# Two buffers for the key tiles of the first attention part, and norm row factors by way of DRAM

## The chip, the cores and the metric

The kernel runs on one core of one Trainium2 chip. The core has five engines that run side by side and are held together by semaphores: TensorE (PE in the profile, its weight loads PEld), VectorE (DVE), ScalarE (ACT), GpSimd (POOL) and SyncE (SP). Here every DMA is issued from SP's queue, in the order in which the program stands there. The metric is the device time of one execution in microseconds (us), as the median of several runs.

## The reference

One layer of a streaming encoder, in float32, for 2048 prompt tokens and 32 sample tokens of width 1024:

```
z  = rmsnorm(x, g_attn) @ w_in            # 3072 columns: q, k, v of two head groups
oa = differential attention, 4 heads:     # softmax(q1 k1) - lam * softmax(q2 k2), chunk-causal, T5 bias
ob = band attention, 8 heads of 64:       # each 64-frame chunk sees itself and the 8 chunks before
h  = x + concat(rmsnorm(oa) * c, rmsnorm(ob)) @ w_out
h  = h + square(relu(rmsnorm(h) @ w_up)) @ w_down
h  = h + sigmoid(h @ w_ple_gate) * (p @ w_ple_proj)
y  = rmsnorm(h)                           # also returned: the new keys and values of both groups
```

The first norm is `x * rsqrt(mean(x*x) + eps) * g`. The factor `rsqrt(...)` is one number for each token, the row factor of this text.

## The kernel before

The tokens are worked on in four blocks of 512 (the last has the 32 sample tokens as well, 544). Activations stand transposed, features on partitions and tokens along the free axis. Each float32 product is made of three fp32r matmuls, from a high and a low part of both operands (`mm3`, lines 215 to 217); ACT makes the high part (line 180) and POOL or DVE the low one (lines 165, 175, 186).

`prep` (line 358) takes a block in tiles of 128 tokens. For each it loads x, squares it on ACT with a running sum, transposes it on TensorE into PSUM tiles `xp` (line 377), takes the high and low parts with the gain `g_attn` (lines 382, 383), copies the plain transposed x away (line 386) and stores it. The norm's factor is not multiplied into the activations. It is worked out in `rsqrt` (lines 219 to 231) into a column of `rcol`, one token on each partition, and used after the projections: the value tiles have tokens on partitions and take `rcol` as the scale of their ACT copy (line 421), while the query and key tiles have tokens along the free axis and need the factors as a row that is the same on all partitions. This is the tile `rb[b]` (`rbt` in the profile, three buffers), read in lines 475 and 480. It is made by a TensorE transpose of the column broadcast to 128 columns (`rp`, line 391), in the PSUM ring that `prep` is given, and an ACT copy into `rb[b]` (line 392), once for each token tile, 17 times in all.

`attn_a` (line 571) is the differential attention. It runs twice: once over queries 0 to 1023 (`JA0`, with `self.small` set, pool `a0`), once over the rest and the sample (`JA1`, pool `a1`). For each of 4 heads it loads a bias tile `ba` (one buffer; a POOL memset follows its load, line 329), the head's keys `kt` (tag `ka`, in two DMAs) and then, for each 256 queries, q tiles, the scores `s` (line 632), the near block's bias and maximum (line 641) or the far block's maximum (line 638), the exponentials (line 646), the weighted difference (lines 668, 669), the transposes `tpp` (line 704), the copies `pH` and `pL` (711, 712), the product with v (`o`, lines 718 to 720) and a norm by column sums (`ss`, lines 729, 730). In the first run `ka` has one buffer of 1024 keys, in the second two of 2048. `attn_b` is the band attention, also in two runs (scores `sb` line 802, transposes `tpb` line 817, product `ob` line 842).

`run` writes this down as: `prep` of blocks 0 and 1 with the first value tiles; the first group's projection for them; `attn_a` over `JA0`; the second group's projection for block 0; `prep(2)` woven into the projection of block 1; the first run of `attn_b`; `prep(3)` woven into the projection of block 2; and so on to the second `attn_b`, the first group's projection of blocks 2 and 3, `attn_a` over `JA1`, the output projection, the MLP and the gate. The order on each engine is not the written one: a scheduler with a timing model of its own takes the instructions by priority and by readiness of their data and buffers, and so mixes the attention with the projections. A change of a buffer count or of a producer can change that order far behind its place. On each engine and on SP's queue the order is fixed once the program is built.

Of the kernel before, what the change touches and what calls it, by code (L numbers as in the profile page):

```python
# [12 lines left out]
F32 = mybir.dt.float32  # L13
F32R = mybir.dt.float32r
AF = mybir.ActivationFunctionType
# [4 lines left out]
P = 128  # L20
D = 1024
SP = 2048
SS = 32
T = SP + SS
# [16 lines left out]
BN = {0: 512, 1: 512, 2: 512, 3: 544}  # L41
# [3 lines left out]
def toks(b):  # L45
    out = []
    for i in range(4):
        out.append((i * P, P))
    if b == 3:
        out.append((512, SS))  # L50
    return out
# [91 lines left out]
class Kern:  # L143
# [197 lines left out]
    def scratch(self):  # L341
        self.xT = self.dram([P, 8, T], F32, "xT")
        self.qS = self.dram([8, 2, 64, 9, 2, 256], F32, "qS")
        self.kS = self.dram([8, 2, P, KC], F32, "kS")
        self.vS = [self.dram([KC, D], F32, "vSa"), self.dram([KC, D], F32, "vSb")]
        self.oT = self.dram([P, 8, T], F32, "oT")
        self.hS = self.dram([P, 8, T], F32, "hS")
        self.rS = self.dram([P, T], F32, "rS")
        self.rB = self.dram([P, T], F32, "rB")
        self.pS = self.dram([P, 2, 2, T], F32, "pS")  # L350

# [6 lines left out]
    def prep(self, b, acts, pp, mm, tag, first=None):  # L358
        nc = self.nc
        aH, aL = acts[b]  # L360
        for i, (c0, n) in enumerate(toks(b)):
            t0 = 512 * b + c0
            x = pp.tile([P, D], F32, tag="x", name="x")
            self.dma(x[:n], self.xsrc(t0, n))
            if first is not None:
                first()
                first = None
            xt = pp.tile([P, 8, P], F32, tag="xt", name="xt")
            st = pp.tile([P, 1], F32, tag="st", name="st")
            nc.scalar.activation(  # L370
                xt[:n].rearrange("p a b -> p (a b)"), x[:n], AF.Square, accum_out=st[:n]
            )
            for h in range(2):
                xp = mm.tile([P, 4, P], F32, tag=tag, name="xp")
                for k in range(4):
                    kk = 4 * h + k
                    nc.tensor.transpose(xp[:, k, :n], x[:n, kk * P : kk * P + P], self.ident[:n, :n])
                for k in range(4):
                    kk = 4 * h + k
                    g = self.g_attn[:, kk : kk + 1]  # L380
                    hi, lo = aH[:, kk, c0 : c0 + n], aL[:, kk, c0 : c0 + n]
                    nc.scalar.activation(hi, xp[:, k, :n], AF.Copy, scale=g)
                    nc.vector.scalar_tensor_tensor(
                        lo, xp[:, k, :n], g, hi.bitcast(F32), op0=ALU.mult, op1=ALU.subtract
                    )
                nc.vector.tensor_copy(xt[:, 4 * h : 4 * h + 4, :n], xp[:, :, :n])
            self.dma(self.xT[:, :, t0 : t0 + n], xt[:, :, :n])
            r = self.rcol[:n, 4 * b + i : 4 * b + i + 1]
            self.rsqrt(pp, st[:n], 1, 1.0 / D, EPS, nc.vector, "r1", n, out=r)
            rp = mm.tile([P, 512], F32, tag=tag, name="rp")  # L390
            nc.tensor.transpose(rp[:, :n], r.broadcast_to([n, P]), self.ident[:n, :n])
            nc.scalar.activation(self.rb[b][:, c0 : c0 + n], rp[:, :n], AF.Copy)
            yield

    def ktok(self, b):
# [175 lines left out]
    def attn_a(self, js, pool, ps_s, ps_t, ps_o):  # L571
        nc = self.nc
        last = 8 in js
        nk = SP if last else 256 * (js[-1] + 1)
        for g in range(4):
            ba = self.bias_a(pool, g)
            kt = pool.tile([P, 2, 1024 if self.small else SP], F32R, tag="ka", bufs=1 if self.small else 2, name="ka")
            if last:
                ks = pool.tile([P, 2, PAST + SS], F32R, tag="ks", bufs=1, name="ks")
            for hl in range(2):  # L580
                src = self.kS[g, hl].rearrange("(m r) c -> r m c", m=2)
                for c0 in range(0, nk, 1024):
                    c1 = min(c0 + 1024, nk)
                    self.dma(kt[64 * hl : 64 * hl + 64, :, c0:c1], src[:, :, c0:c1])
                if last:
                    self.dma(ks[64 * hl : 64 * hl + 64], src[:, :, SP:KC])
            for j in js:
                self.attn_a_pair(g, j if j < 8 else None, kt if j < 8 else ks, ba, pool, ps_s, ps_t, ps_o)
# [981 lines left out]
```

## Time and profile before

| | |
|---|---|
| median of 3 runs | 3191.57 us (3189.75 to 3192.46) |
| profiled execution | 3197.78 us, span 3196.0 us |
| granted TensorE clock, mean | 0.977 |
| TensorE / weight loads busy | 3037.6 us (95%) / 2694.5 us (84%) |
| DVE / ACT / POOL busy | 1851.6 / 1885.5 / 1887.4 us (58%, 59%, 59%) |
| DMA | 521.61 MB, mean 163 GB/s |

A group's row has line, engine, operation, tile written and tiles read, form and count, then busy time with the mean of one in ns, then the engine's idle time just before and what ended it. A row of a wait has who waited for whom, the total in us, how often, and the longest. A row of a tile has the shortest, median and longest duration in ns, and the start of the first and the last. A row of DMA issues has the number, the size of one and the median time from issue to landing. A row of a stretch has its two ends, its length, then each engine's busy time with its instructions, the granted clock, the DMA engines' busy share and GB/s.

### The profile page before, as it was taken

How to read it: one execution, taken by the hardware profiler on the slowest of the kernel's cores; microseconds unless marked ns; L12 is line 12 of the kernel's file. 1: busy time of each engine (PE TensorE's matmuls, PEld its weight loads, DVE VectorE, ACT ScalarE, POOL GpSimd, SP SyncE). 2: the span in 40 equal slices, each digit the busy share in tenths (PEclk: the TensorE clock that was granted, in tenths of full speed). 3: DMA queues.
4: the chain of work that ended last, by engine and by line, in shares of the span. 5: the costliest groups of instructions: out<-in, count | busy, mean ns of one | idle time of the engine just before them, and what ended most of it. 6: DMA issues, size and time to landing. Idle time of an engine off the chain costs nothing.

```text
span 3196.0 us, 53414 instructions
## 1 busy us (share of the span) xinstructions
PE 3037.6 (95%) x18265; PEld 2694.5 (84%) x18265; DVE 1851.6 (58%) x4448; ACT 1885.5 (59%) x4166; POOL 1887.4 (59%) x2572
## 2 busy tenths in 40 slices
PE   8998989999999998999999999998999999899998
PEld 7787877899987787877788888877888888899998
DVE  5157774544454554666765666435577665776663
ACT  5256775766665764676665666554555555554445
POOL 4466546333335544565554555677787778867674
PEclk9998999999999999999999999999999999999999
DMA  8787767977688745555554534446524334233331
GB/s 267 237 242 224 208 191 237 251 227 206 199 244 227 209 130 134 149 165 138 170 158 139 148 111 119 126 147 216 182 86 147 106 99 127 93 100 108 92 114 55
DMA packets 512505, 521.61 MB, mean 163 GB/s; under 512 B 37949, under 2 KB 393601, under 8 KB 512233
## 3 DMA queue, kind: packets, MB, share of 16 engines
q1 hardware_dynamic: 512232, 518.19, 55.2%
q8 instruction: 145, 2.38, 0.3%
q14 instruction: 128, 1.04, 0.1%
HBM read 412.08 MB, written 109.95 MB: 163 GB/s over the span
## 4 chain that ended last, share of the span: by engine, by line
PE 68%; DMA 12%; DVE 10%; ACT 4%; issue 3%; POOL 2%; SPq 1%; DVEq 0%; ACTq 0%; POOLq 0%
PE dps L215 6%; PE dps L216 6%; PE dps L217 6%; PE ups L215 6%; PE ups L216 6%; PE ups L217 6%; PE s L632 3%; PE qps L215 3%; PE qps L216 3%; PE qps L217 3%; DMA oraw<-oT 2%; PE ob L842 2%; PE tpb L817 1%; PE tpp L704 1%; DMA wr<-w_up 1%
## 5 line engine op out<-in xcount | busy, mean ns | idle before, releaser
L175 POOL TENSOR_TENSOR wl<-wr,wh 128x256 fp32r<-128x256 f32 x648 | 474.5, 764 | 333.6 <-ACT wh L180 328.0
L180 ACT ACTIVATE piece<-wr 128x512 fp32r<-128x512 f32 x412 | 252.9, 626 | 289.0 <-PE ups L216 144.0
L175 POOL TENSOR_TENSOR piece<-wr,piece 128x256 fp32r<-128x256 f32 x416 | 336.4, 834 | 103.2 <-ACT piece L180 87.8
L180 ACT ACTIVATE wh<-wr 128x1024 fp32r<-128x1024 f32 x228 | 240.8, 1057 | 198.5 <-PE qps L216 51.7
L165 POOL TENSOR_TENSOR wl<-wr,wh 128x256 fp32r<-128x256 f32 x264 | 197.9, 781 | 185.8 <-ACT wh L180 180.4
L215 PE MATMUL ups<-cs,piece 128*128 128x256 f32 (+1 forms) x896 | 257.3, 288 | 7.8 <-ACT piece L180 6.1
L217 PE MATMUL ups<-cs,piece 128*128 128x256 f32 (+1 forms) x896 | 257.4, 287 | 5.6 <-POOL piece L175 5.6
L216 PE MATMUL ups<-cs,piece 128*128 128x256 f32 (+1 forms) x896 | 256.6, 286 | 0.5 <-DVE cs L186 0.5
L216 PE MATMUL dps<-ul,piece 128*128 128x272 f32 (+1 forms) x768 | 247.7, 324 | 1.3 <-DVE ul L186 1.3
L217 PE MATMUL dps<-uh,piece 128*128 128x272 f32 (+1 forms) x768 | 247.5, 324 | 1.2 <-POOL piece L165 1.2
L215 PE MATMUL dps<-uh,piece 128*128 128x272 f32 (+1 forms) x768 | 246.2, 324 | 1.0 <-DVE h L1124 0.8
L165 POOL TENSOR_TENSOR piece<-wr,piece 128x256 fp32r<-128x256 f32 x280 | 223.5, 829 | 25.1 <-ACT piece L180 24.3
L1124 DVE TENSOR_TENSOR h<-h,dps 128x272 f32<-128x272 f32 (+1 forms) x384 | 190.8, 515 | 81.5 <-PE dps L217 80.5
L215 PE MATMUL qps<-aH,wh 128*128 128x512 f32 (+1 forms) x640 | 230.8, 361 | 5.8 <-DVE ql L475 4.3
L215 PE MATMUL dps<-uh,wh 128*128 128x512 f32 x512 | 209.5, 409 | 20.8 <-ACT wh L180 7.2
L216 PE MATMUL qps<-aL,wh 128*128 128x512 f32 (+1 forms) x640 | 229.2, 358 | 0.0
L217 PE MATMUL qps<-aH,wl 128*128 128x512 f32 (+1 forms) x640 | 228.4, 357 | 0.0
L1083 DVE TENSOR_TENSOR h<-h,dps 128x512 f32<-128x512 f32 x256 | 174.2, 682 | 82.3 <-PE dps L217 77.6
L632 PE MATMUL s<-ka,q 128*128 128x512 f32 (+3 forms) x768 | 188.6, 349 | 19.4 <-DMA ka<-kS 10.0
L215 PE MATMUL ups<-cH,wh 128*128 128x512 f32 x512 | 202.7, 396 | 0.5 <-DVE h L1083 0.4
L216 PE MATMUL dps<-ul,wh 128*128 128x512 f32 x512 | 202.1, 395 | 0.0
L217 PE MATMUL dps<-uh,wl 128*128 128x512 f32 x512 | 202.1, 395 | 0.0
(298 smaller groups left out, 9764.7 us busy)
## 6 DMA issues: line engine op xcount, KB each, us to landing
wr<-w_up SPq DMA_DIRECT2D x128, 512.0 KB, 4.1
wr<-w_down SPq DMA_DIRECT2D x128, 512.0 KB, 3.7
wr<-w_in SPq DMA_DIRECT2D x74, 512.0 KB, 4.6
q<-qS SPq DMA_DIRECT2D x128, 256.0 KB, 5.2
v<-vSa SPq DMA_DIRECT2D x64, 512.0 KB, 3.9
ka<-kS SPq DMA_DIRECT2D x32, 512.0 KB, 7.8
wr<-w_out SPq DMA_DIRECT2D x32, 512.0 KB, 5.0
wr<-w_ple_gate SPq DMA_DIRECT2D x32, 512.0 KB, 4.1
```

The costliest lines, as they stand in the source:

```text
L165: nc.gpsimd.tensor_tensor(out[:, sl], a[:, sl], b[:, sl], op=op)
L175: nc.gpsimd.tensor_tensor(out[:, sl], a[:, sl], b[:, sl], op=op)
L180: nc.scalar.activation(hi, raw, AF.Copy)
L215: nc.tensor.matmul(ps, lh, rh, start=start and i == 0, stop=False)
L216: nc.tensor.matmul(ps, lh, rl, start=False, stop=False)
L217: nc.tensor.matmul(ps, ll, rh, start=False, stop=stop and i == n - 1)
L632: nc.tensor.matmul(s, q[:, m, hl, P * qi : P * qi + nr], kt[:, m, k0 - kb : k0 - kb + n], start=hl == 0, stop=hl == 1)
L704: nc.tensor.transpose(tp[:kn, x, :nr], w[:nr, P * i : P * i + kn], self.ident[:nr, :nr])
L817: nc.tensor.transpose(tp[:kn, x, :nr], e[:, P * (x0 + x) : P * (x0 + x) + kn], self.ident[:nr, :nr])
L842: nc.tensor.matmul(o[:, qa:qb], vt, pt[:kn, i - kfirst, qa:qb], start=x == 0 and y == 0, stop=x == len(order) - 1 and y == 1,)
L1083: nc.vector.tensor_tensor(hv, hv, ps, op=ALU.add)
L1124: nc.vector.tensor_tensor(hv, hv, ps, op=ALU.add)
```

## The change

Two edits. The key tile of the first `attn_a` run gets two buffers, as the second run has. And the rows `rb[b]` are no longer made by transposes: when a block's last token tile is done, the block's columns of `rcol` are written to a DRAM vector `rR` (one token after the other, so in pieces of 4 bytes), and one DMA reads 512 (or 544) factors of it back, repeated on all 128 partitions. The lines behind the first added line move by one, those behind the second edit by eight.

```diff
@@ scratch
+        self.rR = self.dram([T], F32, "rR")
@@ prep
             self.rsqrt(pp, st[:n], 1, 1.0 / D, EPS, nc.vector, "r1", n, out=r)
-            rp = mm.tile([P, 512], F32, tag=tag, name="rp")
-            nc.tensor.transpose(rp[:, :n], r.broadcast_to([n, P]), self.ident[:n, :n])
-            nc.scalar.activation(self.rb[b][:, c0 : c0 + n], rp[:, :n], AF.Copy)
+            if i == len(toks(b)) - 1:
+                self.dma(
+                    self.rR[512 * b : 512 * b + 512].rearrange("(i p) -> p i", p=P), self.rcol[:, 4 * b : 4 * b + 4]
+                )
+                if b == 3:
+                    self.dma(self.rR[SP:T].rearrange("(i p) -> p i", p=SS), self.rcol[:SS, 16:17])
+                self.dma(
+                    self.rb[b][:, : BN[b]],
+                    self.rR[512 * b : 512 * b + BN[b]].unsqueeze(0).broadcast_to([P, BN[b]]),
+                )
             yield
@@ attn_a
-            kt = pool.tile([P, 2, 1024 if self.small else SP], F32R, tag="ka", bufs=1 if self.small else 2, name="ka")
+            kt = pool.tile([P, 2, 1024 if self.small else SP], F32R, tag="ka", bufs=2, name="ka")
```

## The prediction

> **What bounds the kernel now.** I read the page first, then busy time by stretch, then TensorE's waits, then the rows that the change touches.
>
> ```profile
> span 3196.0 us, 53414 instructions
> PE 3037.6 (95%) x18265; PEld 2694.5 (84%) x18265; DVE 1851.6 (58%) x4448; ACT 1885.5 (59%) x4166; POOL 1887.4 (59%) x2572
> PEclk9998999999999999999999999999999999999999
> PE 68%; DMA 12%; DVE 10%; ACT 4%; issue 3%; POOL 2%; SPq 1%; DVEq 0%; ACTq 0%; POOLq 0%
> ```
>
> TensorE is busy for 95% of the span and holds 68% of the chain that ended last. So what counts is (a) TensorE work removed, (b) TensorE's idle time, (c) stretches with a lowered clock. Busy time by stretch (TensorE, weight loads, DVE, ACT, POOL, then granted clock, DMA share, GB/s):
>
> ```profile
> 0.00:180.00 180.00, 160.99 (x912) 135.83 (x913) 60.95 (x169) 71.57 (x181) 73.31 (x110) 0.98 0.78 249
> 180.00:530.00 350.00, 311.92 (x1848) 276.46 (x1848) 231.62 (x732) 237.21 (x683) 216.55 (x313) 0.92 0.74 213
> 530.00:1000.00 470.00, 449.69 (x3154) 416.86 (x3153) 231.40 (x832) 311.59 (x662) 193.26 (x306) 0.99 0.81 232
> 1000.00:2010.00 1010.00, 970.69 (x4991) 818.75 (x4992) 604.67 (x1467) 648.52 (x1464) 539.83 (x765) 0.98 0.53 149
> 2010.00:3196.00 1186.00, 1144.30 (x7365) 1046.59 (x7364) 723.00 (x1250) 616.65 (x1179) 864.40 (x1080) 0.98 0.39 120
> ```
>
> The weakest stretch is 180 to 530 us: the first differential attention part, the second group's projection and the preparation of token blocks 2 and 3 run into each other there. TensorE is idle for 38.1 of 350 us at a clock of 0.92. Both edits work in this stretch or before it.
>
> **The change part by part.** TensorE's waits that the edits touch, or that stand beside them, are these, of the whole run:
>
> ```profile
> PE s L632 <- DMA ka<-kS: 10.0, 4, 3.8
> PE ob L842 <- ACT pHb L826: 7.2, 7, 2.3
> PE rp L391 <- DVE xt L386: 7.1, 6, 2.1
> PE tpp L704 <- DVE e L669: 4.3, 5, 1.4
> PE ss L729 <- DVE sh L182: 3.5, 4, 1.8
> PE ss L729 <- DVE rz L657: 2.3, 1, 2.3
> PE rp L391 <- DVE rcol L230: 2.0, 3, 1.1
> ```
>
> *Row factors, what goes.* 17 transposes on TensorE and 17 copies on ACT:
>
> ```profile
> L391 PE MATMUL rp<-ident,rcol x17: 237/323/477, 10.7 to 526.1; 128*128 128x128 f32 x16, 32*128 32x32 f32 x1
> L392 ACT ACTIVATE rbt<-rp x17: 188/277/313, 11.9 to 526.4; 128x128 f32<-128x128 f32 x16, 128x32 f32<-128x32 f32 x1
> ```
>
> 17 at a median of 0.323 is 5.5 us of TensorE, all of it on the bounding engine: **-5.6** (their exact sum is 5.6). The copies are 17 x 0.277 = 4.7 us on an ACT that is busy 59%: I give them nothing.
>
> Before these transposes TensorE idles 7.1 + 2.0 = 9.1 us. The 2.0 us wait for the factor itself goes. The 7.1 us are a wait for a PSUM slot that the copy of the last input transposes frees; the next projection matmul takes a slot of the same ring and inherits the wait unless other work stands between. In the changed program's order some 20 to 36 attention and projection matmuls stand between the last input transposes and the next projection matmul at most of those places, where 11 to 12 did before the transpose. So I take **-5**, between 0 (all inherited) and -9.1.
>
> *The clock.* The same waits are followed by half-clock spells:
>
> ```profile
> 209.80:213.20 3.40, 3.40 (x18) 3.40 (x18) 1.40 (x10) 0.83 (x5) 1.27 (x2) 0.51 0.84 272
> 291.90:298.50 6.60, 5.04 (x21) 4.98 (x22) 2.35 (x6) 2.07 (x6) 3.12 (x6) 0.50 0.70 223
> 339.60:346.30 6.70, 5.10 (x18) 4.23 (x17) 6.49 (x18) 3.78 (x12) 3.58 (x5) 0.50 0.55 186
> 428.40:435.00 6.60, 5.97 (x27) 5.68 (x27) 5.15 (x20) 3.59 (x13) 0.91 (x1) 0.50 1.05 300
> 459.10:462.30 3.20, 2.96 (x14) 2.99 (x15) 2.53 (x10) 2.21 (x7) 0.73 (x1) 0.50 0.46 156
> 479.60:482.80 3.20, 2.83 (x13) 2.83 (x14) 2.80 (x8) 2.50 (x7) 2.34 (x3) 0.50 0.41 161
> 527.40:530.60 3.20, 3.20 (x9) 2.43 (x9) 0.00 (x0) 0.00 (x0) 0.29 (x2) 0.50 0.88 208
> ```
>
> The first three follow waits for the key tile, the last four waits of the row-factor transposes. What a spell costs is seen in the same matmul at 428.4 to 435.0 us and at 438 to 451 us (full clock), and what began the spell in the rows of TensorE at 428.67 us:
>
> ```profile
> L215 PE MATMUL vps<-wh,aH 128*128 128x256 f32 x7 | 3.1, 438 | 0.4 <-ACT rbt L392 0.4
> ...
> L215 PE MATMUL vps<-wh,aH 128*128 128x256 f32 x12 | 3.5, 288 | 0.0
> ```
>
> ```profile
> 428.67 0.47 PE L391 MATMUL rp<-ident,rcol 128*128 128x128 f32 x1 [1.94 <-DVE xt L386]
> ```
>
> (438 - 288) / 438 = 34% of the spell's busy time. The four spells at the row factors hold 15.0 us of it, 5.1 us lost; I take half, **-2.5** (0 to -5.1). The three at the key tiles hold 13.5 us, 4.6 us lost.
>
> By the Trainium skill (TensorE: Matmul & The Clock Gate, Part 1: The HAM clock gate) the clock is halved only after at least one idle window of about 3.4 us; then none of the waits at the row factors, the longest 2.1 us, would cost clock and the sum would be 2.5 us higher. The trace does not agree: a wait of 1.94 us stands right before a granted clock of 0.50.
>
> *Row factors, what comes.* Nine DMAs on SP's queue: five writes of the factor columns to DRAM in 4-byte pieces (512 for a block), four loads of one row onto 128 partitions. No operation of the trace is the same; the nearest are
>
> ```profile
> g_mlp_s<-g_mlp SPq DMA_DIRECT2D x1, 4.0 KB, 6.4
> rB<-r SPq DMA_DIRECT2D x1, 272.0 KB, 3.0
> rb<-rB SPq DMA_DIRECT2D x3, 256.0 KB, 4.9
> rb<-rB SPq DMA_DIRECT2D x1, 272.0 KB, 8.3
> ```
>
> 1024 pieces of 4 bytes (6.4 us, a read) and the fastest such write to DRAM (3.0) bound the write; the load takes 4.9 to 8.3 us. The round trip is thus 7.9 to 14.7 us. Who needs it is far off:
>
> ```profile
> L475 DVE SCALAR_TENSOR_TENSOR ql<-qps,rbt x19: 677/691/693, 76.1 to 522.8; 128x512 f32<-128x512 f32 x19
> L475 DVE SCALAR_TENSOR_TENSOR ql<-qps,rbt x5: 409/429/441, 608.1 to 657.2; 128x272 f32<-128x272 f32 x5
> L391 PE MATMUL rp<-ident,rcol x1: 274/274/274, 59.5 to 59.5; 128*128 128x128 f32 x1
> ```
>
> Block 1's factors are complete at 59.5 us, so its row is there by some 74.2 if SP is free, before the first use of any row at 76.1; block 3's last transpose is at 526.1 and its first use at 608.1. So the row's lateness costs nothing; that cover would be gone if the round trip passed 16 us in block 1.
>
> The queue is dearer. Each load waits on SP until its write has landed, and all that stands behind it waits too: V and K tile stores (two buffers each), weight, q and v loads. In the changed order 4, 3, 1 and 2 other DMAs stand between write and load of blocks 0 to 3, some 0.5 us each, so SP is held for 3.0 to 6.4 us less 2, 1.5, 0.5 and 1 us: 7 to 20.6 us in all. Two-deep staging hides part (24 matmuls, a V tile, take 3.2 us at this rate):
>
> ```profile
> 60.00:75.00 15.00, 15.00 (x114) 14.12 (x113) 4.86 (x16) 3.74 (x11) 3.02 (x5) 1.00 0.63 205
> ```
>
> I take a quarter of the upper end, **+5** (0 to +20.6).
>
> *Key tiles.* With two buffers the load of the next head's keys no longer waits for the last score matmul of the head before; in the changed order it stands about one head earlier on SP. All four waits, 10.0 us, could go. But the bias tile `ba` keeps one buffer, its load still waits for the head before, and a POOL memset (in order with the weight splits) and then the near-block reduction on DVE wait for it:
>
> ```profile
> ba<-dba SPq DMA_DIRECT2D x8, 128.0 KB, 7.2
> POOL ba L329 <- DMA ba<-dba: 28.8, 8, 8.1
> ```
>
> That is what is late next. In the part with queries 512 to 1023 a head starts with far blocks that need no bias, in the part before it does not. I take **-6** of 10.0 and **-3** of the 4.6 us of clock. Bytes moved are the same.
>
> *The order.* The scheduler lays out anew all that stands before some 1,980 us (up to the 10,754th matmul, and the stretches above count 10,905 up to 2010); after that TensorE's order is the same. Counting TensorE work between producer and consumer (0.27 to 0.38 us a matmul): in the first part, from a query tile's last score matmul to its first transpose, 18.7 us on average where it was 16.2 (smallest 11.5, was 8.4), and before the column sums 2.9 and 5.9 at the smallest, were 2.2 and 3.2. Of the waits there (4.3 + 3.5 + 2.3 = 10.1 us) I take **-4.5** (0 to -10.1). In band attention 11 of 72 places have under 2 us between transposes and their use, 7 before. At 7.2 / 7 = 1.0 us a wait and half a short spell (3.2 x 34% / 2 = 0.5), 4 x 1.5 = **+6** (0 to +13, at the longest wait of 2.3 and a full spell).
>
> **Sum**: -5.6 - 5 - 2.5 + 5 - 6 - 3 - 4.5 + 6 = -15.6 us. The profiled execution took 3197.8 us (1.8 around its span); that gives 3182.2. The median of the runs is 6.2 us below the profiled one, so **3176**. With every term at its best end it is -44.4, with every term at its worst (removed transposes kept) +28.
>
> **Rivals.**
>
> *The bias tile takes the wait over.* Head starts stay where `ba` lands, and the -6, -3 and -4.5 fall away: 3189.5, no change. For it: 28.8 us of POOL idle on it. Against: most key waits fall in heads that begin without bias.
>
> *SP is held by the loads.* All 20.6 us reach TensorE, with a 6.6 us spell for each block (34% of it, 2.2 us, four times): +29.4 in place of +5, so -15.6 + 24.4 = +8.8: 3200. For it: the write and the load of block 2 stand one DMA apart. Against: two-deep staging, and rows that are not needed yet. It is slower by over 0.2% from 27 us on, 6.8 a block.
>
> The Trainium skill (DMA: Bandwidth & Descriptors, Two DMAs through the same engine are not ordered) says that the issuing engine has to wait for the first DMA's semaphore before a DMA that reads what it wrote; the trace of before has such a pair in the second group's norm rows, too far apart to show a wait.
>
> *The new order costs more than it gives (the slower side).* Place: 530 to 1,980 us, band attention beside the projections and the second part beside the MLP. Idle there was 20.3 + 39.3 = 59.6 us. If it grows by two fifths, 23.8 us, in waits of 2 us with a 3.2 us spell each (1.1 us), it is 36.9 us instead of +6: -21.6 + 36.9 = +15.3, 3207. It turns the sign from 14 us more idle and passes 0.2% from 18. For it: the short covers in band attention. Against: score-to-transpose covers of the second part, 21.7 us on average, were 20.9.
>
> *A gain twice as large*: waits and clock of 180 to 530 us fall to half: some -35, 3157.
>
> **How the numbers follow.** Forecast (3160 to 3185) 0.45; larger gain 0.07; the bias tile 0.18; SP held 0.08; the order slower 0.22. A measurement here can tell 0.2%, 6.4 us, from no change. Faster 0.52, within 0.2% 0.18 (bias tile), slower 0.30 (order and SP). The range runs from near the best end to past the slower rival: 3150 to 3212.
>
> **What would show it.** Right: no group for the row-factor transpose; waits for the key tile under 2 us; idle of 180 to 530 us under 30 us and its clock above 0.94; the POOL wait for `ba` still near 28 us; SP waits of 1 to 5 us on the write at four places. Wrong: score matmuls or the near-block reduction waiting for `ba`; value projections waiting for ACT copies or stores just after a row load; band attention's waits for its copies above 15 us; more half-clock spells after 530 us.

## The result, and the profile after

The changed kernel takes 3214.53 us (median of 5 runs, 3212.84 to 3216.36), the kernel before beside it 3192.46: a ratio of 1.0061 with a 95% interval of 1.0047 to 1.0076. It is about 20 us slower, where 3176 (3150 to 3212) was forecast. The profiled execution took 3212.84 us, span 3210.9.

The page of the changed kernel (span, busy time, granted clock by slices):

```profile
span 3210.9 us, 53386 instructions
PE 3036.1 (95%) x18248; PEld 2691.1 (84%) x18248; DVE 1846.6 (58%) x4448; ACT 1883.6 (59%) x4149; POOL 1888.5 (59%) x2572
PEclk9999888999999999999999999999999999999999
```

TensorE's work is 1.5 us less than before (3037.6), and the span is 14.9 us longer: TensorE's idle time grew from 158.4 to 174.8 us. Busy time by stretch of the changed kernel, columns as in the prediction, says where:

```profile
0.00:180.00 180.00, 154.03 (x868) 130.61 (x869) 58.00 (x165) 68.74 (x169) 71.28 (x107) 0.96 0.83 240
180.00:530.00 350.00, 302.15 (x1803) 265.58 (x1802) 222.96 (x718) 227.98 (x659) 204.67 (x297) 0.92 0.76 211
530.00:1000.00 470.00, 446.50 (x3138) 415.80 (x3137) 226.79 (x837) 308.93 (x667) 189.05 (x302) 0.98 0.81 227
1000.00:2010.00 1010.00, 974.41 (x5005) 821.11 (x5004) 604.07 (x1456) 647.16 (x1444) 547.97 (x773) 0.99 0.55 152
2010.00:3210.90 1200.90, 1159.00 (x7442) 1057.99 (x7440) 734.76 (x1273) 630.74 (x1214) 875.56 (x1094) 0.99 0.39 120
```

TensorE's idle time up to 180 us is 26.0 us (19.0 before), from 180 to 530 us 47.9 (38.1 before). Behind 530 us it differs by less than 4 us in any stretch. So the loss falls where the new DMAs stand. TensorE's longest waits up to 560 us, and the new DMAs (number, size, median time from issue to landing):

```profile
PE vps L215 <- ACT vraw L429: 14.6, 4, 7.7
PE xp L378 <- DVE kr L488: 10.1, 1, 10.1
PE tpp L712 <- DVE e L677: 9.0, 4, 5.5
...
PE vps L215 <- DVE xt L387: 3.7, 3, 2.3
PE qps L215 <- DVE xt L387: 3.5, 2, 3.0
```

```profile
rbt<-rR SPq DMA_DIRECT2D x3, 256.0 KB, 3.7
...
rR<-rcol SPq DMA_DIRECT2D x4, 2.0 KB, 10.7
```

The wait for the key tile (10.0 us before) is gone. New are one wait of 7.7 us of a value projection for the copy of the value tile before it, and one of 10.1 us of the input transposes. And a write of 2 KB takes 10.7 us to land. The two long waits stand at two of the four writes. Below are the stretches of 12 us that begin with the writes of blocks 1 and 3 in the changed kernel, and the instructions of its timeline with which DVE and TensorE go on after them (start, duration, engine, line, and in brackets the idle time before and what ended it):

```profile
59.90:71.90 12.00, 5.72 (x51) 5.52 (x49) 1.12 (x5) 1.72 (x5) 0.00 (x0) 0.82 1.14 113
...
507.00:519.00 12.00, 3.03 (x16) 2.22 (x14) 0.00 (x0) 1.31 (x2) 4.75 (x7) 0.83 0.51 91
```

```profile
73.32 0.58 PE L215 MATMUL vps<-wh,aH 128*128 128x256 f32 x1 [7.71 <-ACT vraw L429]
```

```profile
519.13 0.29 DVE L182 CAST cvhl<-cvr 128x256 fp32r<-128x256 f32 x1 [12.20 <-DMA cvr<-cache_b_v]
```

```profile
520.08 1.11 PE L378 MATMUL xp<-ident,x 128*128 128x128 f32 x4 [10.05 <-DVE kr L488]
```

At 507 us nearly the whole core stands still (in the stretch TensorE is busy for 3.0 of 12 us, DVE not at all): DVE waits 12.20 us for `cvr`, a load of cached values that has nothing to do with the row factors but was issued just behind their write, and TensorE waits behind DVE. In these 12 us the DMAs move 91 GB/s, at the write of block 1 113 GB/s with the DMA engines counted as busy all the while.

### The profile page after: what moved, and what is told of

Same layout as the page of the kernel before. It is cut to its first block, busy times and chain, and to the rows that moved or that the text cites. A ratio compares the mean times of both kernels' runs of the same rounds, so it can differ in the third digit from the quotient of the medians.

```text
span 3210.9 us, 53386 instructions
## 1 busy us (share of the span) xinstructions
PE 3036.1 (95%) x18248; PEld 2691.1 (84%) x18248; DVE 1846.6 (58%) x4448; ACT 1883.6 (59%) x4149; POOL 1888.5 (59%) x2572
```

## The experiments

Four theories: **W**, the write of 4-byte pieces itself holds every DMA that stands behind it; **S**, SP is held because the row's load must wait for the write; **O**, the new order of the instructions costs the time; **K**, the second key buffer does. Unless said otherwise, a ratio is against the kernel before on the same chip, with its 95% interval. In the diffs `...` stands for lines that are not shown.

**One edit at a time.** The kernel before with two buffers for `ka`:

```diff
-tag="ka", bufs=1 if self.small else 2, name="ka")
+tag="ka", bufs=2, name="ka")
```

> Only the key tile gets its second buffer; the row factors are made by transposes as before. Theory W (the write of the row factors in 4-byte pieces holds every DMA issued behind it for about 10 us, and TensorE with it): the loss is in the other edit, so this kernel is at 3180 to 3195 us, with the waits for the key tile under 2 us. Rival O (the re-laid order costs the time, whatever moved it): this kernel is re-laid as far as the changed one is, so 3205 to 3220.

Measured: 3188.38 us, ratio 0.9993 [0.9981, 1.0004]. The changed kernel with `ka` as before:

```diff
-tag="ka", bufs=2, name="ka")
+tag="ka", bufs=1 if self.small else 2, name="ka")
```

> Only the row factors go by way of DRAM; the key tile keeps one buffer. Theory W: 3205 to 3225 us, four writes that land after about 10 us each, and what is issued just behind them lands as late. Rival O: TensorE's order moves by about 4,000 of 18,245 matmuls (in the changed kernel 5,100), so part of the loss, 3200 to 3212. Rival K (the second key buffer is what costs): 3185 to 3195.

Measured: 3220.38 us, ratio 1.009 [1.007, 1.0111]. K falls; the rows bring the whole loss.

**The write by itself.** The kernel before, transposes kept, plus the four block writes; nothing reads them, so nothing waits for them:

```diff
+        self.rR = self.dram([T], F32, "rR")
...
+            if i == len(toks(b)) - 1:
+                self.dma(
+                    self.rR[512 * b : 512 * b + 512].rearrange("(i p) -> p i", p=P), self.rcol[:, 4 * b : 4 * b + 4]
+                )
```

> The kernel before, with the four writes of a block's factor columns to DRAM in 4-byte pieces added and nothing else: transposes kept, nothing reads what is written, nothing waits for it on SP. TensorE's order differs from the one before in 6 matmuls. Theory W: the writes alone cost, 3203 to 3225 us, each landing after about 10 us. Rival S (SP's queue held by the row load that waits for the write is the cost, as in the prediction): no load, so 3190 to 3196. Rival O: 3190 to 3196.

Measured: 3220.57 us, ratio 1.0087 [1.0067, 1.0106], landing 10.3 us. All but 6 matmuls stand in the order of before, no load waits, and the loss is as large as with the whole edit. So neither O nor S is needed for it. What is it about this write? Other forms of it, at the same four places (the first diff is against the one just shown, the next two are against the kernel before). Each partition's four factors side by side, in one piece of 16 bytes:

```diff
-        self.rR = self.dram([T], F32, "rR")
+        self.rR = self.dram([4, P, 4], F32, "rR")
...
-                self.dma(
-                    self.rR[512 * b : 512 * b + 512].rearrange("(i p) -> p i", p=P), self.rcol[:, 4 * b : 4 * b + 4]
-                )
+                self.dma(self.rR[b], self.rcol[:, 4 * b : 4 * b + 4])
```

> The kernel before with the four writes added as in the run with the write alone, but each in 128 pieces of 16 bytes in place of 512 of 4; the order of every engine is the same as in that run. The write alone in 4-byte pieces took 3220.6 us against 3190.4. If the number of pieces sets the cost: landing after 2.5 to 5 us, time 3188 to 3197. If any such write holds the queue, whatever its pieces: 3210 to 3222.

One column only, so a quarter of the pieces:

```diff
...
+self.dma(self.rR[512 * b : 512 * b + P].rearrange("(p i) -> p i", i=1), self.rcol[:, 4 * b + 3 : 4 * b + 4])
```

> As the run with the write alone, but only the last of a block's four columns is written: 128 pieces of 4 bytes, side by side in DRAM. If the number of pieces sets the cost (some 20 ns a piece for 512 in 10 us): landing after 4 to 5 us, time 3190 to 3199. If the 4-byte size itself is the trouble (an own slow way for such writes): landing still near 8 to 10 us, 3205 to 3220.

All pieces, with gaps between them in DRAM: 512 bytes from one to the next as shown, then 16 and 8 with a last size of 4 and 2 in place of the last `P`:

```diff
+        self.rR = self.dram([4, 4, P, P], F32, "rR")
...
+                self.dma(self.rR[b, :, :, 0].rearrange("i p -> p i"), self.rcol[:, 4 * b : 4 * b + 4])
```

> As the run with the write alone, 512 pieces of 4 bytes a block, but each piece 512 bytes from the next in DRAM in place of side by side; same order. If several DMA engines writing into the same stretch of DRAM get in each other's way: landing after 3 to 6 us, 3188 to 3200. If each 4-byte piece costs by itself: landing after some 10 us as before, 3212 to 3226.

> The kernel before plus four writes of a block's factor columns, 512 pieces of 4 bytes each as in the write-only run, but each piece begins 16 bytes behind the last (nothing reads what is written; the order on TensorE and SP is that of the write-only run). If pieces disturb each other only where they touch or lie within one 16-byte unit, the write lands in 2 to 3.5 us and the time is that of before, 3190 (3186 to 3196), as with pieces of 16 bytes side by side. If they disturb each other within a larger unit (64 to 512 bytes), it lands in 5 to 11 us and the time is 3200 to 3222. If the size of the pieces mattered after all: 3220.

> The kernel before plus four writes of a block's factor columns in 512 pieces of 4 bytes, each piece beginning 8 bytes behind the last (nothing reads them; order as in the write-only run). If pieces disturb each other only where they touch: 3190 (3186 to 3196), landing 2 to 3.5 us. If they do within a unit of 16 bytes, with two pieces in one: 3198 to 3222, landing 5 to 11 us.

| one write | landing, median us | ratio to before |
|---|---|---|
| 512 pieces of 4 bytes, touching | 10.3 | 1.0087 [1.0067, 1.0106] |
| 128 pieces of 4 bytes, touching | 8.2 | 1.0078 [1.0061, 1.0095] |
| 512 of 4 bytes, 8 bytes apart | 5.2 | 1.0022 [1.0008, 1.0035] |
| 512 of 4 bytes, 16 bytes apart | 3.4 | 1.0006 [0.9995, 1.0018] |
| 512 of 4 bytes, 512 bytes apart | 2.5 | 1.0008 [0.9995, 1.0021] |
| 128 of 16 bytes, touching | 2.9 | 1.0013 [1.0002, 1.0024] |

I had expected the number of pieces to set the cost; the second and fifth rows refute it. A quarter of the pieces is nearly as dear, and the full number costs nothing when they stand apart. It isn't the size either, since 4-byte pieces 16 bytes apart are harmless. Nor is it the way the DMA is cut up: the four forms of 512 pieces all have 514616 DMA packets on their pages. What costs is that 4-byte pieces, here from neighbouring partitions, stand beside each other in DRAM, and it fades from touching over 8 to 16 bytes. (At 8 bytes the two medians, 3206.93 and 3195.26, stand further apart than the ratio says; either way it lies between its neighbours.)

TensorE and SP have the same order of instructions in the touching run and in the run with 16 bytes between the pieces, so their traces can be laid over each other (they are from two chips, on which the kernel before took 3190.41 and 3189.19 us). First the touching one, the 12 us from each write on; then the other:

```profile
28.50:40.50 12.00, 9.11 (x56) 8.88 (x56) 6.04 (x14) 6.11 (x17) 7.06 (x10) 0.72 1.20 152
60.40:72.40 12.00, 9.88 (x87) 9.68 (x86) 2.87 (x10) 3.25 (x11) 1.54 (x3) 1.00 1.04 124
369.00:381.00 12.00, 9.65 (x61) 8.27 (x59) 4.44 (x12) 4.87 (x15) 7.44 (x12) 1.00 0.24 41
507.00:519.00 12.00, 4.98 (x30) 4.28 (x29) 0.93 (x3) 2.18 (x3) 1.71 (x4) 0.79 0.34 52
```

```profile
27.70:39.70 12.00, 9.77 (x61) 9.74 (x61) 7.64 (x19) 8.97 (x25) 7.78 (x11) 0.72 1.02 287
55.70:67.70 12.00, 12.00 (x108) 12.00 (x108) 6.63 (x20) 5.44 (x16) 2.91 (x4) 1.00 0.60 199
360.50:372.50 12.00, 11.56 (x73) 10.00 (x72) 9.23 (x26) 10.36 (x32) 11.26 (x17) 1.00 0.78 232
489.90:501.90 12.00, 9.52 (x58) 7.83 (x57) 4.73 (x11) 4.76 (x9) 6.99 (x10) 1.00 0.77 237
```

The last column is GB/s: 152, 124, 41 and 52 with touching pieces, 287, 199, 232 and 237 with gaps. TensorE works 33.6 of these 48 us in the one and 42.9 in the other. The DMAs that were issued in the first of these stretches and have nothing to do with the factors are late too (a weight tile and value tile stores; touching first):

```profile
wr<-w_in SPq DMA_DIRECT2D x1, 512.0 KB, 11.0
vSa<-vhl SPq DMA_DIRECT2D x2, 256.0 KB, 11.0
```

```profile
wr<-w_in SPq DMA_DIRECT2D x1, 512.0 KB, 5.2
vSa<-vhl SPq DMA_DIRECT2D x2, 256.0 KB, 5.1
```

The input transposes and the gate's matmuls (shortest, median and longest duration, first and last start) show how late the same work is, again the touching run first:

```profile
L378 PE MATMUL xp<-ident,x x136: 220/273/475, 4.6 to 547.6; 128*128 128x128 f32 x128, 32*128 32x32 f32 x8
...
L215 PE MATMUL gps<-hu,piece x128: 388/396/399, 2297.0 to 2762.8; 128*128 128x512 f32 x128
```

```profile
L378 PE MATMUL xp<-ident,x x136: 220/273/446, 4.6 to 523.8; 128*128 128x128 f32 x128, 32*128 32x32 f32 x8
...
L215 PE MATMUL gps<-hu,piece x128: 388/396/399, 2269.2 to 2735.4; 128*128 128x512 f32 x128
```

It is 23.8 us late right behind the last write, 27.4 to 27.8 in the gate, and the spans end 28.0 apart (3220.7 and 3192.7). Nothing is given back. Four writes at 10.3 - 3.4 us give 27.6: in this pair nearly all of the longer landing ends up in the span.

**The changed kernel with a harmless write.** Its own order on TensorE, row written in 16-byte pieces:

```diff
-self.rR[512 * b : 512 * b + 512].rearrange("(i p) -> p i", p=P), self.rcol[:, 4 * b : 4 * b + 4]
+self.rR[512 * b : 512 * b + 512].rearrange("(p i) -> p i", p=P), self.rcol[:, 4 * b : 4 * b + 4]
```

The reads stay as they are, so the factors reach the wrong tokens.

> The changed kernel with one difference: a block's factors go to DRAM in 128 pieces of 16 bytes, one a partition, in place of 512 of 4 bytes. The row then holds the factors in another order of the tokens, so that the queries and keys of a block are scaled by the factors of other tokens. The order of all engines and of SP is the same. Theory W, if the cost goes with the number of pieces: writes land after 3 to 5 us and the time is 3185 to 3200. Rival O, or a key tile that costs: 3211 to 3217, the changed kernel's own time. Rival S: between, some 3205, as SP is held for a shorter time.

Measured: 3186.8 us, ratio 0.9984 [0.997, 0.9997]. Once more on another chip, with the changed kernel itself beside it (first the changed kernel):

> The changed kernel once more, beside its form with 16-byte pieces on the same chip. If the write is the loss wherever it runs: 3210 to 3222, ratio 1.006 to 1.009. If the loss was the chip's: 3190 to 3200.

> The changed kernel with the row written in 16-byte pieces, once more (factors in another token order than the reads take them, same order of instructions on TensorE). If the write of touching pieces is the whole loss: 3182 to 3194, ratio 0.997 to 1.001, and 20 to 30 us under the changed kernel. If the read or the order takes a part on this chip: 3196 to 3207.

Measured: 3218.14 us, ratio 1.006 [1.0044, 1.0077], against 3192.07 us, ratio 0.9988 [0.9977, 0.9999]. TensorE has the same order in both. The only difference is the layout of a block's 2 KB in DRAM, and it is worth 26 us. SP's waits for the write up to 545 us, in the changed kernel and in the first run with 16-byte pieces:

```profile
SPq L156 <- DMA rR<-rcol: 27.3, 4, 9.6
```

```profile
SPq L156 <- DMA rR<-rcol: 8.8, 4, 2.8
```

A form that keeps the tokens in order: the four columns are transposed together and the row is written as four runs of 512 bytes.

```diff
...
+                rw = pp.tile([4, 160], F32, tag="rw", bufs=1, name="rw")
+                nc.tensor.transpose(rp[:4, :P], self.rcol[:, 4 * b : 4 * b + 4], self.ident)
+                nc.scalar.activation(rw[:, :P], rp[:4, :P], AF.Copy)
+                self.dma(self.rR[512 * b : 512 * b + 512].rearrange("(i p) -> i p", p=P), rw[:, :P])
...
```

> Both edits, but a block's four factor columns are transposed together (one transpose of 128x4, one small copy) and written to DRAM as four rows of 512 bytes; the load is as in the changed kernel. The result is the kernel's own again. Theory W: no hold of the queue, writes land after 2.5 to 5 us: 3175 to 3195; TensorE does 5 row-factor transposes in place of 17. Rival O: the order is laid out anew once more, 8,919 of 18,250 matmuls moved, so 3195 to 3215.

Measured: 3190.38 us, ratio 1.0003 [0.9989, 1.0016]. No loss, and no gain. The changed kernel with no write at all, its row tiles loaded from a row of the input:

```diff
...
-self.rR[512 * b : 512 * b + BN[b]].unsqueeze(0).broadcast_to([P, BN[b]]),
+self.a["x_prompt"][0, b, : BN[b]].unsqueeze(0).broadcast_to([P, BN[b]]),
```

> The changed kernel without the writes of the factors: the row tiles are filled by the same repeated load from a row of the input instead (so the factors are wrong numbers), and nothing holds SP for a write. If the write is the whole loss and the held queue costs little: 3180 to 3194, within 5 us of the run with 16-byte pieces. If the repeated read itself costs as the write did: 3205 to 3220. The prediction gave the held queue 5 us: then this is 5 us under the run with 16-byte pieces.

Measured: 3200.1 us, ratio 1.0011 [1.0001, 1.0022]. This lies in neither expected range, and is slower than the run that writes, 3192.07, on the same chip. At some 2,300 of 18,248 places in TensorE's order another matmul stands than in the changed kernel. The new order is the likely reason for the 0.2%, but that was not shown, and the price of the held queue can't be read from this pair.

**Attempts at a better kernel.** 16-byte pieces put back into token order by an ACT copy (`rbt` viewed as `(i p)`, the read tile `rq` as `(p i)`, four copies of 1.1 us):

```diff
...
+                nc.scalar.activation(
+                    self.rb[b][:, :512].rearrange("q (i p) -> q i p", p=P),
+                    rq[:, :512].rearrange("q (p i) -> q i p", i=4),
+                    AF.Copy,
+                )
...
```

> The changed kernel with the row written token by partition, so in 128 pieces of 16 bytes side by side, read back in that order into a spare buffer of the key ring (kr), and put into token order by one ACT copy a block (512 elements, some 0.6 us) into the row tile. If the write of 4-byte pieces is the whole of the loss, the time is at most that of before: 3187 (3176 to 3196), and the write lands in 2.5 to 5 us. If the read repeated on all partitions, the held queue or the second key buffer's order holds a part of the loss, 3200 to 3215. The order differs from that of both kernels, which alone was worth up to 6 us in earlier runs.

Measured: 3196.13 us, ratio 1.0018 [1.0005, 1.0032], just above the lower of the two ranges. The same without the copies for blocks 0 to 2, where the multiplication reads the row with a step of four:

```diff
...
+                            rb = rb.rearrange("q (p i) -> q i p", i=4)
...
-                                r_, ps[:, :n], 0.125, rb, op0=ALU.mult, op1=ALU.mult
+                                v(r_), v(ps[:, :n]), 0.125, rb, op0=ALU.mult, op1=ALU.mult
```

> The changed kernel with the row written in 128 pieces of 16 bytes, token by partition, and read back in that order; for blocks 0 to 2 the multiplication behind the projection reads the row with a step of four elements, for block 3 two ACT copies put it into token order. TensorE's order is that of the changed kernel in all but 1278 of 18245 instructions. If the loss lay in the 4-byte pieces side by side alone, the time is that of the run with 16-byte pieces and the same order: 3187 (3178 to 3192), ratio below 1. If the order behind the edit decides as much as what was edited, as in the run with the ACT copies, 3190 to 3200. If the held queue or the repeated read holds the loss, 3205 to 3215.

Measured: 3211.6 us, ratio 1.0047 [1.003, 1.0064]. This missed. The write is harmless in it (median landing 3.9 us). What its profile shows is the price of the step:

```profile
L496 DVE SCALAR_TENSOR_TENSOR ql<-qps,rbt x40: 424/1060/1142, 82.2 to 916.8; 128x512 f32<-128x512 f32 x24, 128x272 f32<-128x272 f32 x16
```

A multiplication of 512 columns takes 1.06 us where it took 0.69. It stands between the projection's PSUM slot and the next projection. But the profile caught the fastest of six executions (3194.93 us, the slowest 3217.51), so it doesn't show where the others lose; that stays open. Last, no DRAM at all: the kernel before with a block's four row transposes in one PSUM tile and one copy.

```diff
...
+                for j in range(4):
+                    rj = self.rcol[:, 4 * b + j : 4 * b + j + 1]
+                    nc.tensor.transpose(rp[:, P * j : P * j + P], rj.broadcast_to([P, P]), self.ident)
+                nc.scalar.activation(self.rb[b][:, :512], rp, AF.Copy)
...
```

> The kernel before with the four row transposes of a block put into one PSUM tile at the block's last token tile and copied by one ACT instruction of 512 columns: the same TensorE work, 5 copies and 5 PSUM slots in place of 17, no DRAM. The prediction gave 5 us to the waits before these transposes and 2.5 us to the clock there; if those terms hold without the DRAM way, about three quarters of them come: 3184 (3180 to 3190). If the waits are inherited by the next projection matmul, no change: 3190.

Measured: 3197.18 us, ratio 1.0023 [1.001, 1.0036], slower than either expectation. The wait for the PSUM slot didn't go; the value projection has it now (before: 7.1 us at `rp`):

```profile
PE vps L215 <- DVE xt L386: 7.9, 4, 3.6
```

No version that keeps the tokens in order is faster than the kernel before; the second key buffer alone is equal to it.

## Why the prediction was wrong

**The step that failed** is the bound of the write: "1024 pieces of 4 bytes (6.4 us, a read) and the fastest such write to DRAM (3.0) bound the write". It lands after 10.7 us. Neither row was of its kind: the read scatters over partitions and the write goes in long runs. A price without a row of its kind was bounded as if the two nearest enclosed it. **The second** is what is held: the prediction let SP alone be held, for 7 to 20.6 us, of which two-deep staging hides three quarters. SP's waits for the write came to 27.3 us, but they aren't the mechanism: the write-only run has no waiting load and loses as much, because the DMAs behind the write crawl at 41 to 152 GB/s. Staging did not cover 10 us in which little lands. The term of +5 measures +26 (the pair on one chip) to +28 (the overlaid traces).

The other terms can be read in the second run with 16-byte pieces, which has the changed kernel's order on TensorE and SP waits of 8.7 us in place of 27.3. Its ratio makes -3.8 us, its profiled span is 3189.9 us, 6.1 less than before, where the prediction's sum without the +5 for the queue was -20.6. Its stretches and waits (waits of the whole run):

```profile
0.00:180.00 180.00, 165.38 (x941) 140.61 (x942) 60.45 (x169) 73.64 (x177) 77.24 (x116) 0.98 0.83 259
180.00:530.00 350.00, 306.29 (x1819) 268.50 (x1818) 231.46 (x753) 235.37 (x684) 211.24 (x309) 0.93 0.78 218
...
sum 3189.90, PE 3033.22 PEld 2688.80 DVE 1850.12 ACT 1887.53 POOL 1891.96; mean PE 606.64 PEld 537.76 DVE 370.02 ACT 377.51 POOL 378.39
```

```profile
PE sb L810 <- DVE stb L813: 5.7, 6, 3.5
PE s L640 <- DVE nm L649: 5.6, 7, 2.3
PE s L640 <- ACT e L654: 5.1, 6, 1.8
PE s L640 <- DMA q<-qS: 4.0, 2, 3.3
...
PE vps L215 <- DVE xt L387: 3.9, 3, 2.5
PE qps L215 <- DVE xt L387: 3.5, 2, 3.0
```

- *17 transposes, -5.6*: it fits. TensorE's busy time is 4.4 us less (3037.6 to 3033.2).
- *The waits before them, -5 of 9.1*: wrong. 3.9 + 3.5 = 7.4 us stand now at the next value and query projections, for the same copy `xt`. The prediction named this end ("all inherited") and argued it away with 20 to 36 matmuls in between. The longest wait, 3.03 us, has none in between; but one of 2.46 us comes behind 33 of them, because DVE, in its own order, began the copy only at 456.25 us, 9 us after the transposes. So counting TensorE's work is not enough. The batched run says the same (7.9).

```profile
456.98 0.58 PE L215 MATMUL vps<-wh,aH 128*128 128x256 f32 x1 [2.46 <-DVE xt L387]
...
498.37 0.76 PE L215 MATMUL qps<-aH,wh 128*128 128x512 f32 x1 [3.03 <-DVE xt L387]
```

- *The clock, -2.5 and -3*: did not come. 180 to 530 us has 0.93 where it had 0.92, and the mean is 0.977 in both.
- *Key tiles, -6*: the waits for `ka` are gone as said, but the scores wait for the next thing: 5.6 + 5.1 + 4.0 us and 0.4 more for maxima, exponentials, q and v tiles, 15.1 us in all. Before, all waits of `s` were 19.3 (10.0 of them for `ka`). With the key buffer alone they are 20.8. The -6 is 4 in the one, none in the other.
- *The order, -4.5 and +6*: both of the wrong sign. The first part's transposes wait more (`tpp` and `ss`: 9.6 us up to 560 us before, 10.3 now), the band part's scores, transposes and products less (22.4 to 17.6, loads included). Places counted with a short cover did not foretell either.
- *Nobody waits for the row*: right. Apart from SP's queue (0.7 us) nothing waits for the loads of `rbt`; their first use in the changed kernel is at 93.5 us, moved with the projection.
- *The bias tile takes the wait over*: in part, as the rival and one of the signs of being wrong said. Before, no instruction of DVE waits for the tile's memset; with 16-byte pieces the near-block reduction does, for 9.9 us (14.0 in the changed kernel, 6.7 with the key buffer alone). Three of the seven score waits for the maxima, 3.8 of their 5.6 us, stand right behind such a wait; the longest is the last row below. POOL's own wait for the load does not show it: up to 560 us it is 18.6 us, where it was 28.8.

```profile
POOL ba L329 <- DMA ba<-dba: 18.6, 7, 5.5
...
DVE e L649 <- POOL ba L329: 9.9, 5, 3.3
...
204.84 0.29 DVE L649 CUSTOM_DVE_ANT_0 e<-s,ba 128x128 f32<-128x128 f32 x1 [3.33 <-POOL ba L329]
...
205.19 0.39 PE L640 MATMUL s<-ka,q 128*128 128x256 f32 x1 [2.29 <-DVE nm L649]
```

Of the rivals, "SP is held by the loads" (3200) has the right place and the wrong mechanism; the slower side that the prediction preferred, the new order from 530 to 1980 us, did not occur: the stretches behind 530 us stand as before. With the queue's term taken out, 4 us came of 20.6, as much as the transposes alone save. TensorE's idle time was 158.4 us and is 156.7: waits that were taken away came back under other names. One reading of the prediction doesn't hold either: it said that the second group's norm rows lie too far apart to show a wait, but in the trace of before SP waits once for their write (`rB<-r`), 3.5 us.

The Trainium skill (DMA: Bandwidth & Descriptors, Specifications) states that below 512 bytes the DMA does a read-modify-write. All forms in the table have pieces below that, so it alone does not tell them apart. The runs do: 4-byte pieces 512 bytes apart land in 2.5 us, touching ones in 10.3.

## What to carry to other kernels

A column with one element on each partition should not be written to DRAM as a row of touching 4-byte pieces: transpose it first, or let each partition write at least 16 bytes, or let the pieces begin at least 16 bytes apart. Look at what a DMA does to the DMAs behind it, not only at who waits for it; here no waiter named the write in TensorE's list, and GB/s in the 12 us behind it did. And when a wait of an engine that is 95% busy is taken away, price it at nothing until the next releaser in line is known to be early.

## What the hardware showed that I had not expected

In the write-only run the core's DMAs moved 41 to 152 GB/s in the 12 us from a 2 KB write on, and the landing went with the distance of the pieces in DRAM (10.3, 5.2, 3.4 and 2.5 us at 4, 8, 16 and 512 bytes), hardly with their number (8.2 us for a quarter).

```profile
rR<-rcol SPq DMA_DIRECT2D x4, 0.5 KB, 8.2
```

```profile
rR<-rcol SPq DMA_DIRECT2D x4, 2.0 KB, 2.5
```

The first row is the run with one column, the second that with all pieces 512 bytes apart. That small pieces close together in DRAM get in each other's way is what the runs show. Whether it matters that they come from different partitions, and which part of the way to DRAM makes them wait, was not tried. All times were taken beside the kernel's other traffic.
